# Layer 0's attention: each head's scaling and output transposes emitted inside the next head's tiles

## The chip, the core and the metric

The kernel runs on one core of a Trainium2 chip. The core has five engines that work side by side, each from a queue of its own: TensorE (PE, with its weight loads as PEld), VectorE (DVE), ScalarE (ACT), GpSimd (POOL) and SyncE (SP). They wait for each other through semaphores, and DMA engines move data between HBM, where the inputs lie, and the on-chip memory (SBUF). TensorE writes its results to PSUM. The metric is the device time of one execution in microseconds, the median of several runs.

## The reference, cut to what matters

The program is a two-layer backbone over 256 context and 512 latent tokens (T = 768, D = 1024). Layer 0 mixes tokens with two head groups side by side: four heads of differential attention, and four heads of a gated delta rule (GDN). The change lies in the attention heads and in what is done beside them:

```python
def _diff_attend(q, k, v, lam):
    s = jnp.einsum('bqhmd,bkhmd->bhmqk', q, k).astype(jnp.float32) * (A_HD ** -0.5)
    p = jax.nn.softmax(s, axis=-1)
    w = p[:, :, 0] - lam * p[:, :, 1]
    return jnp.einsum('bhqk,bkhe->bqhe', w.astype(v.dtype), v)

def merge(oa, ob, gate, ref):
    ya = (_rmsnorm(oa, subln_g) * (1.0 - lam_init)).reshape(bsz, n, A_V)
    yb = (_rmsnorm(ob, out_g) * jax.nn.silu(gate)).reshape(bsz, n, B_W)
    return jnp.concatenate([ya.astype(ref.dtype), yb.astype(ref.dtype)], axis=-1) @ w_out
```

Each attention head has two score maps; their softmaxes are subtracted with weight lambda and multiplied with V. Each head's output is then RMS-normed over its 128 columns. The GDN heads' output is normed too and multiplied with a gate, and both groups go through one output projection. Context queries see only the 256 context keys, latent queries see all 768.

## The kernel before, in words

Activations are held feature-major: a tile of 128 features on the partitions and 768 tokens along the free axis. Float32 projections are made of three passes over a value split in a high and a low part (`mm3`, L346, L347, L349); the weight's split is made on the fly by `wload` (L333 ACT for the high part, L335 DVE or POOL for the low part).

`layer0_mixer` first runs the GDN, which leaves its output in `self.O`, then the q, k and V projections of attention, and then the part that is touched here. PSUM holds there three large buffers (tag `big`: the scores `sc`, the transposed output `oT`, a gate's projection `pj`, the broadcasts `hb`) and two small ones (`sml`: `pT`, `pav`, `hn`).

For each of the four heads `attn_load` (L989) brings q and k from DRAM with twelve DMAs on POOL's queue into tiles with twelve buffers, six for one head. `attn_head` (L615) then loops over six tiles of 128 queries, the four latent ones (768 keys) first and the two context ones (256 keys) behind. One tile is: scores of both maps on TensorE (L633, L634), their maximum on DVE (L635), the exponential with its sum on ACT (L637, into one of five `e` buffers), three DVE instructions that combine both maps (L639, L641, L642), six transposes on TensorE (L647) with copies on ACT (L648), six products with V (L651), and a copy to `ot` on ACT (L652). POOL copies the first map's reciprocal to `r0` (L640).

Behind the six tiles stands the head's scaling: squares on POOL (L654, into an `e` buffer), row sums on DVE (L655), two POOL multiplies with `r0`, `rpow` on DVE (L564: an inverse square root by three integer steps and four Newton rounds of three instructions), a POOL multiply (L659) and POOL's scaling pass over the whole head (L660). Then the output: six transposes on TensorE into `oT` (L663) and the split into high and low part on ACT and DVE (L666, L667).

Behind head 0 comes `headnorm` (L578) for the GDN output, in two sets of two heads: squares on ACT, row sums as 24 matmuls a set (L588), `rpow` on DVE, 24 broadcasts a set (L595). Then come gates 0 and 1, and behind head 1 gates 2 and 3: a projection of u (48 passes of `mm3` over 384 columns), a tanh on ACT (L1091), a combination on DVE (L1092) and a product into `self.O` on POOL (L1093). Head 2 is preceded by the split of the four finished O tiles (L381 ACT, L382 DVE). Behind head 3 the residual x is loaded and the output projection `out0` begins.

The framework gives each engine its queue: it takes the emitted order as priority and lets a later instruction go first where its own estimates say that the earlier one isn't ready; buffers of one tag are handed out in turn. On the chip each queue then runs in that fixed order.

Of the kernel before, what the change touches and what calls it, by code (L numbers as in the profile page):

```python
# [18 lines left out]
P = 128  # L19
D = 1024  # L20
KT = D // P
NC = 256
NL = 512
T = NC + NL
NCH = T // P
# [218 lines left out]
class K:  # L244
# [319 lines left out]
    def rpow(self, x):  # L564
        nc = self.nc
        n = x.shape[-1]
        w = self.nwt.tile([P, 2, n], F32, tag="nwt", name=self.nm("nwt"), bufs=2)
        y, t = w[:, 0, :], w[:, 1, :]
        I32 = mybir.dt.int32
        nc.vector.tensor_scalar(x, x, 1.0 / P, EPS, op0=ALU.mult, op1=ALU.add)  # L570
        nc.vector.tensor_scalar(t.bitcast(I32), x.bitcast(I32), 1, None, op0=ALU.logical_shift_right)
        nc.vector.tensor_scalar(y.bitcast(I32), t.bitcast(I32), -1, 0x5F3759DF, op0=ALU.mult, op1=ALU.add)
        for i in range(4):
            nc.vector.tensor_tensor(t, y, y, op=ALU.mult)
            nc.vector.scalar_tensor_tensor(t, t, -0.5, x, op0=ALU.mult, op1=ALU.mult)
            nc.vector.scalar_tensor_tensor(x if i == 3 else y, t, 1.5, y, op0=ALU.add, op1=ALU.mult)

    def headnorm(self, os, nrm, gain):  # L578
        nc = self.nc
# [32 lines left out]
        self.sg = self.small(1, "sg")  # L612
        nc.vector.tensor_scalar(self.sg, self.sm("subln"), 1.0 - lam_init, None, op0=ALU.mult)

    def attn_head(self, h, qk, Vh, ypool, pool, ae, **kw):  # L615
        nc = self.nc
        ident = self.c("ident")
        o = pool.tile([P, NCH, P], F32, tag="ot", name=self.nm("ot"), bufs=2)
        rs = pool.tile([P, 2, NCH], F32, tag="rs", name=self.nm("rs"), bufs=2)
        r0, ss = rs[:, 0, :], rs[:, 1, :]  # L620
        for qt in (2, 3, 4, 5, 0, 1):
            k1 = T if qt >= 2 else NC
            nkt = k1 // P
            wt = pool.tile([P, NCH, P], F32, tag="wT", name=self.nm("wT"), bufs=NWT)
            es = []
            st = pool.tile([P, 6], F32, tag="st", name=self.nm("st"), bufs=8)
            for m in range(2):
                ps = self.big("sc")
                q, k, kl = qk[3 * m:3 * m + 3]
                lq = q[:, qt * P:qt * P + P]  # L630
                for a in range(0, k1, 512):
                    b = min(a + 512, k1)
                    nc.tensor.matmul(ps[:, a:b], lq, k[:, a:b], start=True, stop=False)  # L633
                    nc.tensor.matmul(ps[:, a:b], lq, kl[:, a:b], start=False, stop=True)  # L634
                nc.vector.reduce_max(st[:, m:m + 1], ps[:, 0:k1], axis=AX.X, negate=True)  # L635
                e = ae.tile([P, T], F32, tag="e", name=self.nm("e"), bufs=NE)
                nc.scalar.activation(e[:, 0:k1], ps[:, 0:k1], AF.Exp, bias=st[:, m:m + 1], accum_out=st[:, 2 + m:3 + m])  # L637
                es.append(e)
            nc.vector.reciprocal(st[:, 4:6], st[:, 2:4])  # L639
            nc.gpsimd.tensor_copy(r0[:, qt:qt + 1], st[:, 4:5])  # L640
            nc.vector.tensor_scalar(st[:, 5:6], st[:, 5:6], st[:, 2:3], self.nlam, op0=ALU.mult, op1=ALU.mult)  # L641
            nc.vector.scalar_tensor_tensor(es[0][:, 0:k1], es[1][:, 0:k1], st[:, 5:6], es[0][:, 0:k1], op0=ALU.mult, op1=ALU.add)  # L642
            for g in range(0, nkt, 3):
                gn = min(3, nkt - g)
                pt = self.sml("pT")
                for j in range(gn):
                    nc.tensor.transpose(pt[:, j * P:j * P + P], es[0][:, (g + j) * P:(g + j + 1) * P], ident)  # L647
                nc.scalar.activation(wt[:, g:g + gn, :], pt[:, 0:gn * P].rearrange("p (a b) -> p a b", a=gn), AF.Copy)  # L648
            po = self.sml("pav")
            for kt in range(nkt):  # L650
                nc.tensor.matmul(po[:, 0:P], wt[:, kt, :], Vh[:, kt * P:kt * P + P], start=kt == 0, stop=kt == nkt - 1)  # L651
            nc.scalar.activation(o[:, qt, :], po[:, 0:P], AF.Copy)  # L652
        sq = ae.tile([P, T], F32, tag="e", name=self.nm("sq"), bufs=NE).rearrange("p (a b) -> p a b", a=NCH)
        nc.gpsimd.tensor_tensor(sq, o, o, op=ALU.mult)  # L654
        nc.vector.tensor_reduce(ss, sq, axis=AX.X, op=ALU.add)  # L655
        nc.gpsimd.tensor_tensor(ss, ss, r0, op=ALU.mult)
        nc.gpsimd.tensor_tensor(ss, ss, r0, op=ALU.mult)
        self.rpow(ss)
        nc.gpsimd.tensor_tensor(ss, ss, r0, op=ALU.mult)  # L659
        nc.gpsimd.tensor_tensor(o, o, ss.unsqueeze(2).to_broadcast([P, NCH, P]), op=ALU.mult)  # L660
        pb = self.acc("oT", halves=True)
        for c in range(NCH):
            nc.tensor.transpose(pb[:, c * P:c * P + P], o[:, c, :], ident)  # L663
        yh = self.slot([P, T], F32R, "h", ypool, **kw)
# [351 lines left out]
    def layer0_mixer(self):  # L1016
        nc, tc = self.nc, self.tc
        w0 = self.ap["w0"]
        with ExitStack() as es:
# [52 lines left out]
            with self.psum("ps1", big=3, sml=2), tc.tile_pool(name="at", bufs=1, reuse_waits="tile") as at, \  # L1072
                    tc.tile_pool(name="ae", bufs=1, reuse_waits="tile") as ae:
                self.nwt = at
                ya = []
                yt = lambda tag, n, pool=at: pool.tile([P, T], F32, tag=tag, name=self.nm(tag), bufs=n)
                yt2 = lambda tag: at.tile([P, 2, T], F32, tag=tag, name=self.nm(tag), bufs=1)
                hg = self.small(1, "hg")
                nc.vector.tensor_scalar(hg, self.sm("gnorm"), 0.5, None, op0=ALU.mult)
                for h in range(4):  # L1080
                    qk = self.attn_load(h, at)
                    if h == 2:
                        ya += [self.split(self.O[:, i, :], pool=self.sp) for i in range(4)]
# [12 lines left out]

# [280 lines left out]
AD0 = 1  # L1377
AD1 = 7
OH = 0
GATES = ((0, 1), (2, 3), (), ())  # L1380
NQK = 12
NE = 5
NWT = 3
# [39 lines left out]
```

## Time and profile before

| | us |
|---|---|
| median of three runs | 2017.19 |
| lowest and highest run | 2016.58, 2025.78 |
| the profiled execution, its own time | 2019.74 |
| span of the profiled execution, first to last instruction | 2017.9 |
| mean granted clock of TensorE | 0.939 |
| layer 0's attention stage in the span | 512.2 to 703.6 |

Times in the trace are counted from the span's start. "Busy" is the time in which an engine works on an instruction. A granted clock of 1.00 is TensorE's higher level, 2.4 GHz, and 0.5 its lower one, 1.2 GHz; a stretch with both has a value between them. A wait is put down to the instruction that released it.

### The profile page before, as it was taken

The numbers are of one execution on the slowest core, as the hardware profiler recorded it, in microseconds if no ns is written. First come the engines' busy times: TensorE is split into PE (matmuls) and PEld (weight loads), VectorE is DVE, ScalarE is ACT, GpSimd is POOL, SyncE is SP. The second block draws the span as 40 slices with busy tenths as digits, with TensorE's granted clock in tenths as the row PEclk, the third lists the DMA queues.
The fourth block names the chain that finished last, engine by engine and source line by source line (L and its number), as shares of the span: only waits on it lengthen the run. The fifth ranks groups of instructions, "written<-read, shape, count | busy, mean of one in ns | idle before, by whom it ended". The sixth has DMA issues, their size and how long they took to land. (4 is left out here: it accounts for less than half of the span.)

```text
span 2017.9 us, 27188 instructions
## 1 busy us (share of the span) xinstructions
PE 1826.2 (90%) x10129; PEld 1599.8 (79%) x10129; DVE 1299.4 (64%) x2440; ACT 878.0 (44%) x1630; POOL 522.8 (26%) x410
## 2 busy tenths in 40 slices
PE   7588898989787698999999999989888999999997
PEld 2477788888686487999999999967566688888887
DVE  4898887985455437665765544677666685555556
ACT  4355543343434335442333242365666464333344
POOL 1545312221322114322222222233121331111112
PEclk9788977997798799999999999989999999999998
DMA  8433222222523024333344344333000242333324
GB/s 313 136 125 112 79 92 84 84 97 56 132 57 100 0 84 126 117 94 103 126 136 146 105 131 131 100 99 110 27 21 17 70 129 86 113 94 94 94 79 121
DMA packets 75669, 202.87 MB, mean 101 GB/s; under 512 B 8545, under 2 KB 18961, under 8 KB 75153
## 3 DMA queue, kind: packets, MB, share of 16 engines
q1 hardware_dynamic: 65984, 173.01, 27.4%
q10 hardware_dynamic: 4752, 16.85, 2.5%
q0 software_dynamic: 4800, 11.28, 2.5%
q8 instruction: 80, 1.31, 0.3%
q14 instruction: 53, 0.43, 0.1%
HBM read 189.28 MB, written 9.99 MB: 99 GB/s over the span
## 5 line engine op out<-in xcount | busy, mean ns | idle before, releaser
L333 ACT ACTIVATE hi<-raw 128x512 fp32r<-128x512 f32 (+2 forms) x429 | 262.0, 616 | 461.0 <-PE pj L347 209.6
L346 PE MATMUL pj<-uh,hi 128*128 128x384 f32 (+1 forms) x1248 | 437.1, 350 | 16.5 <-DVE cv L435 11.6
L347 PE MATMUL pj<-ul,hi 128*128 128x384 f32 (+1 forms) x1248 | 435.3, 349 | 0.0
L335 POOL TENSOR_TENSOR lo<-raw,hi 128x512 fp32r<-128x512 f32 (+1 forms) x143 | 193.7, 1354 | 725.1 <-ACT hi L333 687.6
L349 PE MATMUL pj<-uh,lo 128*128 128x384 f32 (+1 forms) x1248 | 344.5, 350 | 1.8 <-DVE lo L335 0.9
L335 DVE TENSOR_TENSOR lo<-raw,hi 128x512 fp32r<-128x512 f32 (+2 forms) x286 | 209.7, 737 | 166.6 <-ACT hi L333 156.1
L346 PEld LDWEIGHTS pj<-uh,hi 128*128 128x128 f32 x1248 | 243.4, 195 | 22.0 <-issue 16.5
L347 PEld LDWEIGHTS pj<-ul,hi 128*128 128x128 f32 x1248 | 243.4, 195 | 3.2 <-issue 0.8
L349 PEld LDWEIGHTS pj<-uh,lo 128*128 128x128 f32 x1248 | 233.5, 195 | 7.2 <-POOL lo L335 1.8
L435 DVE SCALAR_TENSOR_TENSOR y<-pj,smt,y 128x511 f32<-128x511 f32 (+1 forms) x264 | 161.6, 655 | 58.6 <-ACT y L425 56.1
L346 PE MATMUL dn<-h,hi 128*128 128x384 f32 (+2 forms) x560 | 193.0, 345 | 2.8 <-ACT hi L333 2.3
L347 PE MATMUL dn<-l,hi 128*128 128x384 f32 (+2 forms) x560 | 192.5, 344 | 0.0
L349 PE MATMUL dn<-h,lo 128*128 128x384 f32 (+2 forms) x560 | 168.2, 344 | 1.5 <-DVE lo L335 1.2
L560 DVE SCALAR_TENSOR_TENSOR x<-dn,mod,x 128x512 f32<-128x512 f32 (+1 forms) x152 | 93.0, 633 | 87.2 <-PE dn L349 87.1
L346 PE MATMUL pj<-u,hi 128*128 128x512 f32 x336 | 130.7, 389 | 0.0
L347 PE MATMUL pj<-u,hi 128*128 128x512 f32 x336 | 130.7, 389 | 0.0
L349 PE MATMUL pj<-u,lo 128*128 128x512 f32 x336 | 130.7, 389 | 0.0
L520 ACT ACTIVATE srow<-srow 128x1024 f32<-128x1024 f32 x56 | 59.3, 1059 | 154.2 <-POOL srow L519 149.3
L519 POOL TENSOR_TENSOR srow<-ada1w,srow 128x1024 f32<-128x1024 f32 x32 | 79.1, 2473 | 177.0 <-DMA ada1w<-in_ada 126.0
L346 PEld LDWEIGHTS dn<-h,hi 128*128 128x128 f32 x560 | 105.7, 189 | 10.6 <-ACT hi L333 3.7
L347 PEld LDWEIGHTS dn<-l,hi 128*128 128x128 f32 x560 | 105.7, 189 | 7.0 <-issue 0.5
L349 PEld LDWEIGHTS dn<-h,lo 128*128 128x128 f32 x560 | 103.5, 189 | 9.3 <-DVE lo L335 1.7
(410 smaller groups left out, 3351.2 us busy)
## 6 DMA issues: line engine op xcount, KB each, us to landing
raw<-in_wu SPq DMA_DIRECT2D x88, 512.0 KB, 3.6
ada1w<-in_ada SPq DMA_DIRECT2D x48, 512.0 KB, 3.6
raw<-in_w SPq DMA_DIRECT2D x38, 512.0 KB, 3.7
raw<-in_wd SPq DMA_DIRECT2D x72, 256.0 KB, 2.7
adaw<-in_ada0t ACTq DMA_DIRECT2D x24, 512.0 KB, 3.6
qk<-qdr POOLq DMA_DIRECT2D x48, 192.0 KB, 3.3
adaw<-in_ada SPq DMA_DIRECT2D x16, 512.0 KB, 7.6
raw<-in_w0o SPq DMA_DIRECT2D x16, 512.0 KB, 3.6
```

What stands on the lines that cost most here:

```text
L333: nc.scalar.activation(hi, raw[:, a:b], AF.Copy)
L335: eng.tensor_tensor(lo, raw[:, a:b], hi.bitcast(F32), op=ALU.subtract)
L346: nc.tensor.matmul(ps, hi[n], xh[:, a:b], start=n == 0, stop=False)
L347: nc.tensor.matmul(ps, hi[n], xl[:, a:b], start=False, stop=False)
L349: nc.tensor.matmul(ps, lo[n], xh[:, a:b], start=False, stop=n == last)
L435: nc.vector.scalar_tensor_tensor(y[:, o0:o1], ps[:, o0 + s:o1 + s], taps[i], y[:, o0:o1], op0=ALU.mult, op1=ALU.add)
L519: nc.gpsimd.tensor_tensor(junk, raw, self.srow[:, 0, :], op=ALU.mult)
L520: nc.scalar.activation(junk, junk, AF.Copy, accum_out=col(0))
L560: nc.vector.scalar_tensor_tensor(xs[m][:, a:b], ps[:, a:b], self.mod[l][0 if a >= NC else 1][:, 8 * mi + m:8 * mi + m + 1], xs[m][:, a:b], ...
```

## The change

`attn_head` is cut in three: `attn_tile` (one tile of queries), `attn_scale` and `attn_out`. Head h's scaling is emitted behind the second tile of head h + 1, its transposes and output split behind the fourth. Head 3's follow behind the loop. q and k of head h + 1 are loaded ahead of head h's tiles. One gate each stands behind heads 0 and 1, and gates 2 and 3 behind head 2; the split of O moves ahead of head 3. In the scaling, POOL's copies of `r0` go (the reciprocal is written to `rs` at once), the three small POOL multiplies move to DVE, and `rpow` makes three Newton rounds, in `headnorm` too.

```diff
-        for i in range(4):
+        for i in range(3):
             nc.vector.tensor_tensor(t, y, y, op=ALU.mult)
             nc.vector.scalar_tensor_tensor(t, t, -0.5, x, op0=ALU.mult, op1=ALU.mult)
-            nc.vector.scalar_tensor_tensor(x if i == 3 else y, t, 1.5, y, op0=ALU.add, op1=ALU.mult)
+            nc.vector.scalar_tensor_tensor(x if i == 2 else y, t, 1.5, y, op0=ALU.add, op1=ALU.mult)
...
-    def attn_head(self, h, qk, Vh, ypool, pool, ae, **kw):
-        rs = pool.tile([P, 2, NCH], F32, tag="rs", name=self.nm("rs"), bufs=2)
-        r0, ss = rs[:, 0, :], rs[:, 1, :]
-        for qt in (2, 3, 4, 5, 0, 1):
...
-            nc.vector.reciprocal(st[:, 4:6], st[:, 2:4])
-            nc.gpsimd.tensor_copy(r0[:, qt:qt + 1], st[:, 4:5])
-            nc.vector.tensor_scalar(st[:, 5:6], st[:, 5:6], st[:, 2:3], self.nlam, op0=ALU.mult, op1=ALU.mult)
-            nc.vector.scalar_tensor_tensor(es[0][:, 0:k1], es[1][:, 0:k1], st[:, 5:6], es[0][:, 0:k1], op0=ALU.mult, op1=ALU.add)
...
+    def attn_tile(self, qt, qk, Vh, o, rs, pool, ae):
...
+        nc.vector.reciprocal(rs[:, qt, :], st[:, 2:4])
+        nc.vector.tensor_scalar(st[:, 4:5], rs[:, qt, 1:2], st[:, 2:3], self.nlam, op0=ALU.mult, op1=ALU.mult)
+        nc.vector.scalar_tensor_tensor(es[0][:, 0:k1], es[1][:, 0:k1], st[:, 4:5], es[0][:, 0:k1], op0=ALU.mult, op1=ALU.add)
...
+    def attn_scale(self, o, rs, pool, ae):
+        nc = self.nc
+        r0 = rs[:, :, 0]
+        f = pool.tile([P, NCH], F32, tag="st", name=self.nm("f"), bufs=8)
         sq = ae.tile([P, T], F32, tag="e", name=self.nm("sq"), bufs=NE).rearrange("p (a b) -> p a b", a=NCH)
         nc.gpsimd.tensor_tensor(sq, o, o, op=ALU.mult)
-        nc.vector.tensor_reduce(ss, sq, axis=AX.X, op=ALU.add)
-        nc.gpsimd.tensor_tensor(ss, ss, r0, op=ALU.mult)
-        nc.gpsimd.tensor_tensor(ss, ss, r0, op=ALU.mult)
-        self.rpow(ss)
-        nc.gpsimd.tensor_tensor(ss, ss, r0, op=ALU.mult)
-        nc.gpsimd.tensor_tensor(o, o, ss.unsqueeze(2).to_broadcast([P, NCH, P]), op=ALU.mult)
+        nc.vector.tensor_reduce(f, sq, axis=AX.X, op=ALU.add)
+        nc.vector.tensor_tensor(f, f, r0, op=ALU.mult)
+        nc.vector.tensor_tensor(f, f, r0, op=ALU.mult)
+        self.rpow(f)
+        nc.vector.tensor_tensor(f, f, r0, op=ALU.mult)
+        nc.gpsimd.tensor_tensor(o, o, f.unsqueeze(2).to_broadcast([P, NCH, P]), op=ALU.mult)
+
+    def attn_out(self, o, ypool, **kw):
+        nc = self.nc
         pb = self.acc("oT", halves=True)
         for c in range(NCH):
-            nc.tensor.transpose(pb[:, c * P:c * P + P], o[:, c, :], ident)
+            nc.tensor.transpose(pb[:, c * P:c * P + P], o[:, c, :], self.c("ident"))
         yh = self.slot([P, T], F32R, "h", ypool, **kw)
         yl = self.slot([P, T], F32R, "l", ypool, **kw)
         nc.scalar.activation(yh, pb, AF.Copy, scale=self.sg)
...
+                qk2 = self.attn_load(0, at)
                 for h in range(4):
-                    qk = self.attn_load(h, at)
-                    if h == 2:
+                    if h == 3:
                         ya += [self.split(self.O[:, i, :], pool=self.sp) for i in range(4)]
-                    ya.append(self.attn_head(h, qk, V[h], ae if h < 2 else self.sp, at, ae, **({"bufs": 4} if h < 2 else {})))
+                    qk, qk2 = qk2, self.attn_load(h + 1, at) if h < 3 else None
+                    o = at.tile([P, NCH, P], F32, tag="ot", name=self.nm("ot"), bufs=2)
+                    rs = at.tile([P, NCH, 2], F32, tag="rs", name=self.nm("rs"), bufs=2)
+                    for n, qt in enumerate((2, 3, 4, 5, 0, 1)):
+                        self.attn_tile(qt, qk, V[h], o, rs, at, ae)
+                        if h and n == 1:
+                            self.attn_scale(*prev, at, ae)
+                        if h and n == 3:
+                            ya.append(self.attn_out(prev[0], *((self.sp,) if h > 2 else (ae,)), **({} if h > 2 else {"bufs": 4})))
+                    prev = o, rs
                     if h == OH:
                         for i in (0, 2):
                             self.headnorm([self.O[:, i + k, :] for k in range(2)], yt2("nrm"), hg)
...
                         nc.scalar.activation(gt, ps, AF.Tanh, scale=0.5)
                         nc.vector.scalar_tensor_tensor(gt, gt, 1.0, ps, op0=ALU.add, op1=ALU.mult)
                         nc.gpsimd.tensor_tensor(self.O[:, j, :], self.O[:, j, :], gt, op=ALU.mult)
+                self.attn_scale(*prev, at, ae)
+                ya.append(self.attn_out(prev[0], self.sp))
                 xs = self.loadx(self.sp)
                 nb = Norm(self, xs, lambda sh, dt, nm: yt("e", NE, ae), NS[1])
 
...
-GATES = ((0, 1), (2, 3), (), ())
+GATES = ((0,), (1,), (2, 3), ())
```

## Rows read from the trace of the kernel before

**Rows 1.** The page's busy times by engine, whole span.

```profile
PE 1826.2 (90%) x10129; PEld 1599.8 (79%) x10129; DVE 1299.4 (64%) x2440; ACT 878.0 (44%) x1630; POOL 522.8 (26%) x410
```

**Rows 2.** Attention stage by stretch: length; PE, PEld, DVE, ACT, POOL busy; clock; DMA.

```profile
512.20:542.30 30.10, 21.88 (x129) 18.43 (x127) 15.88 (x30) 15.33 (x41) 11.12 (x26) 0.83 0.72 163
542.30:565.30 23.00, 16.36 (x105) 16.19 (x103) 12.66 (x52) 2.75 (x4) 6.69 (x11) 0.63 0.24 55
565.30:582.00 16.70, 16.70 (x99) 16.70 (x98) 3.35 (x4) 2.72 (x5) 3.13 (x2) 1.00 0.11 33
582.00:605.10 23.10, 19.70 (x126) 15.94 (x124) 15.96 (x31) 16.18 (x41) 8.81 (x16) 1.00 0.37 92
605.10:615.60 10.50, 1.63 (x9) 1.45 (x8) 3.51 (x16) 0.28 (x1) 5.61 (x9) 0.55 0.32 75
615.60:634.10 18.50, 18.50 (x98) 18.50 (x98) 3.36 (x4) 3.60 (x6) 3.14 (x2) 0.89 0.10 29
634.10:660.80 26.70, 19.86 (x125) 16.65 (x124) 20.93 (x36) 18.97 (x45) 3.59 (x7) 0.94 0.39 138
660.80:670.40 9.60, 1.30 (x8) 1.17 (x7) 3.46 (x16) 0.28 (x1) 3.54 (x5) 0.67 0.00 0
670.40:694.30 23.90, 21.84 (x126) 17.46 (x124) 16.02 (x31) 15.99 (x41) 1.11 (x6) 0.92 0.00 1
694.30:703.60 9.30, 1.12 (x5) 1.12 (x6) 3.46 (x16) 0.20 (x1) 3.54 (x5) 0.53 0.00 0
512.20:703.60 191.40, 138.87 (x810) 123.61 (x809) 98.58 (x236) 76.29 (x183) 50.28 (x89) 0.83 0.28 73
```

**Rows 3.** TensorE's waits, 500 to 745 us (total, times, longest).

```profile
PE oT L663 <- POOL ot L660: 31.2, 4, 8.9
```

**Rows 4.** Timeline behind the last head, 694 to 706 us (start, length).

```profile
694.57 1.47 POOL L654 TENSOR_TENSOR sq<-ot 128x768 f32<-128x768 f32 x1 [5.92 <-ACT ot L652]
696.07 0.95 DVE L655 TENSOR_REDUCE rs<-sq 128x6 f32<-128x768 f32 x1 [6.84 <-POOL sq L654]
697.62 0.17 DVE L570 TENSOR_SCALAR rs<-rs 128x6 f32<-128x6 f32 x1 [0.59 <-POOL rs L657]
700.44 0.17 DVE L576 SCALAR_TENSOR_TENSOR rs<-nwt 128x6 f32<-128x6 f32 x1
700.96 1.47 POOL L660 TENSOR_TENSOR ot<-ot,rs 128x768 f32<-128x768 f32 x1
702.48 1.54 PE L663 MATMUL oT<-cst,ot 128*128 128x128 f32 x6 [8.30 <-POOL ot L660]
704.06 0.90 ACT L666 ACTIVATE h<-oT,sg 128x768 fp32r<-128x768 f32 x1 [9.56 <-PE oT L663]
704.99 1.02 DVE L667 SCALAR_TENSOR_TENSOR l<-oT,sg,h 128x768 fp32r<-128x768 f32 x1 [4.39 <-ACT h L666]
```

**Rows 5.** Timeline of the stretch behind head 0, 542 to 566 us.

```profile
542.26 2.94 PE L588 MATMUL hn<-cst,nrm 128*128 128x1 f32 x24
546.13 5.28 PE L588 MATMUL hn<-cst,nrm 128*128 128x1 f32 x24 [0.93 <-ACT nrm L585]
555.17 1.94 DVE L574 TENSOR_TENSOR nwt<-nwt 128x12 f32<-128x12 f32 x1
555.58 1.49 POOL L660 TENSOR_TENSOR ot<-ot,rs 128x768 f32<-128x768 f32 x1
557.12 1.54 PE L663 MATMUL oT<-cst,ot 128*128 128x128 f32 x6 [5.71 <-POOL ot L660]
558.46 7.08 PE L595 MATMUL hb<-cst,hst 128*128 128x128 f32 x48
```

**Rows 6.** Timeline of POOL and DVE inside head 1, 584 to 597 us.

```profile
584.82 1.84 POOL L1093 TENSOR_TENSOR O<-O,gt 128x768 f32<-128x768 f32 x1 [0.95 <-DVE gt L1092]
585.86 1.82 DVE L635 TENSOR_REDUCE st<-sc 128x1 f32<-128x768 f32 x2 [0.25 <-PE sc L634]
595.87 0.57 POOL L998 DMA_DIRECT2D qk<-qdr  x1 [2.79 <-PE sc L634]
```

More of the change, by code (lines that the diff above doesn't have):

```diff
@@ L613, in lam_prep @@
         nc.vector.tensor_scalar(self.sg, self.sm("subln"), 1.0 - lam_init, None, op0=ALU.mult)
-    def attn_head(self, h, qk, Vh, ypool, pool, ae, **kw):
+    def attn_tile(self, qt, qk, Vh, o, rs, pool, ae):
         nc = self.nc
         ident = self.c("ident")
-        o = pool.tile([P, NCH, P], F32, tag="ot", name=self.nm("ot"), bufs=2)
-        rs = pool.tile([P, 2, NCH], F32, tag="rs", name=self.nm("rs"), bufs=2)
-        r0, ss = rs[:, 0, :], rs[:, 1, :]
-        for qt in (2, 3, 4, 5, 0, 1):
[L622 to L638, printed above, removed]
-            nc.vector.reciprocal(st[:, 4:6], st[:, 2:4])
-            nc.gpsimd.tensor_copy(r0[:, qt:qt + 1], st[:, 4:5])
-            nc.vector.tensor_scalar(st[:, 5:6], st[:, 5:6], st[:, 2:3], self.nlam, op0=ALU.mult, op1=ALU.mult)
-            nc.vector.scalar_tensor_tensor(es[0][:, 0:k1], es[1][:, 0:k1], st[:, 5:6], es[0][:, 0:k1], op0=ALU.mult, op1=ALU.add)
[L643 to L652, printed above, removed]
@@ new lines, in attn_tile @@
+        k1 = T if qt >= 2 else NC
+        nkt = k1 // P
+        wt = pool.tile([P, NCH, P], F32, tag="wT", name=self.nm("wT"), bufs=NWT)
+        es = []
+        st = pool.tile([P, 6], F32, tag="st", name=self.nm("st"), bufs=8)
+        for m in range(2):
+            ps = self.big("sc")
+            q, k, kl = qk[3 * m:3 * m + 3]
+            lq = q[:, qt * P:qt * P + P]
+            for a in range(0, k1, 512):
+                b = min(a + 512, k1)
+                nc.tensor.matmul(ps[:, a:b], lq, k[:, a:b], start=True, stop=False)
+                nc.tensor.matmul(ps[:, a:b], lq, kl[:, a:b], start=False, stop=True)
+            nc.vector.reduce_max(st[:, m:m + 1], ps[:, 0:k1], axis=AX.X, negate=True)
+            e = ae.tile([P, T], F32, tag="e", name=self.nm("e"), bufs=NE)
+            nc.scalar.activation(e[:, 0:k1], ps[:, 0:k1], AF.Exp, bias=st[:, m:m + 1], accum_out=st[:, 2 + m:3 + m])
+            es.append(e)
@@ new lines, in attn_tile @@
+        nc.vector.reciprocal(rs[:, qt, :], st[:, 2:4])
+        nc.vector.tensor_scalar(st[:, 4:5], rs[:, qt, 1:2], st[:, 2:3], self.nlam, op0=ALU.mult, op1=ALU.mult)
+        nc.vector.scalar_tensor_tensor(es[0][:, 0:k1], es[1][:, 0:k1], st[:, 4:5], es[0][:, 0:k1], op0=ALU.mult, op1=ALU.add)
+        for g in range(0, nkt, 3):
+            gn = min(3, nkt - g)
+            pt = self.sml("pT")
+            for j in range(gn):
+                nc.tensor.transpose(pt[:, j * P:j * P + P], es[0][:, (g + j) * P:(g + j + 1) * P], ident)
+            nc.scalar.activation(wt[:, g:g + gn, :], pt[:, 0:gn * P].rearrange("p (a b) -> p a b", a=gn), AF.Copy)
@@ L653, in attn_head @@
+        po = self.sml("pav")
+        for kt in range(nkt):
+            nc.tensor.matmul(po[:, 0:P], wt[:, kt, :], Vh[:, kt * P:kt * P + P], start=kt == 0, stop=kt == nkt - 1)
+        nc.scalar.activation(o[:, qt, :], po[:, 0:P], AF.Copy)
+    def attn_scale(self, o, rs, pool, ae):
+        nc = self.nc
+        r0 = rs[:, :, 0]
+        f = pool.tile([P, NCH], F32, tag="st", name=self.nm("f"), bufs=8)
         sq = ae.tile([P, T], F32, tag="e", name=self.nm("sq"), bufs=NE).rearrange("p (a b) -> p a b", a=NCH)
```

## The prediction

> **What bounds the kernel now.** I read four views, from wide to narrow. The busy times say that TensorE is the engine that counts: 90% of the span, VectorE 64% [rows 1]. So a change pays where TensorE stands still, and every us taken from it here arrives at the end, because the stages behind this one keep it as busy. Next, the same busy times for the attention stage alone, cut by hand at the places where TensorE's work changes [rows 2]: 191.4 us, TensorE busy for 138.9, granted clock 0.83. The ten stretches are, in order: head 0's tiles (30.1), the head norm with head 0's output transposes (23.0), gates 0 and 1 (16.7), head 1's tiles (23.1), head 1's scaling (10.5), gates 2 and 3 (18.5), head 2's tiles (26.7), its scaling (9.6), head 3's tiles (23.9), its scaling (9.3). In the scaling stretches TensorE does 1.1 to 1.6 us of work, in the gates it is never idle. Third, TensorE's waits: 31.2 us in four waits of the oT transposes for POOL's scaled head [rows 3]; no other wait of the stage comes near. Fourth, the timeline of one such wait [rows 4]: square on POOL (1.47), row sums on DVE (0.95), POOL multiplies, fifteen small DVE instructions from 697.62 to 700.61 at 0.20 each, POOL again, POOL's scaling pass (1.47), and at 702.48 the transposes, 8.3 us after TensorE stopped. It is one serial chain over two engines, and TensorE's queue holds oT in front of everything else.
>
> **The change, part by part.**
>
> *The three inner chains leave TensorE's queue.* Heads 0 to 2 get their scaling emitted behind tile 1 of the next head and their transposes behind tile 3. The stretches of 10.5 and 9.6 [rows 2] go whole: -20.1. Their six transposes come back inside the next head: 1.5 us at the lower clock [rows 4], half that at the higher; I take 1.0 for each of three heads: +3.0. In front of oT there now lie a gate and two to four tiles, so the chain (about 8 us by [rows 4]) has cover: a gate is 16.7/2 = 8.35 us of pure TensorE work in which DVE is busy for 3.35/2 = 1.7 us [rows 2]. If the cover is gone, see the slow rival.
>
> *Head norm.* Its second set of row sums ends at 551.4, its broadcasts start at 558.46; between lie the oT wait and the transposes [rows 5]. Without head 0's scaling, the broadcasts wait only for the second set's power: a copy and now 12 instructions (three Newton rounds, not four) at 0.20, from 551.45 to about 554.1. That saves 558.46 - 554.1 = 4.4. Ends: 1.3, if the scaling is still woven in there and only the transposes go; 7.1, if the first set's broadcasts start at 551.4 (that set's sums end at 545.2, so its power could be there at about 548). I take 4.4, the middle of the three.
>
> *Gates.* One behind head 0, one behind head 1, two behind head 2. The work is the same; 18.5 us at clock 0.89 against 16.7 at 1.00 [rows 2] says that the 10.5 us pause before it cost 1.8. With that pause gone: -1.8. Each gate's DVE, ACT and POOL work stays beside TensorE's.
>
> *The split of O* moves from head 2's start to head 3's. Head 2 takes 26.7 against head 1's 23.1, with DVE busy 20.9 against 16.0 [rows 2]; the 3.6 move along: 0. Head 3's 23.9 falls to head 1's 23.1 without the pause in front of it: -0.8. The loads of x and the output weights come after u is free, a head later than now, but still a head (over 20 us) before their first use: 0.
>
> *Loads of q and k.* Head 2's are already issued while head 1's tiles run [rows 6], and no wait for a later head's load stands in TensorE's list. Being a head ahead buys nothing: 0. What is queued behind them on POOL is the square; TensorE does not wait for it at that point.
>
> *The POOL copies of r0* (24) and the POOL multiplies go; DVE has three more small instructions per head. Unhidden only behind head 3: three Newton instructions fewer (-0.6) and fewer crossings, POOL's two multiplies taking 697.02 to 697.62 against 2 x 0.20, the last one 700.61 to 700.96 against 0.20 plus a crossing [rows 4]: about -0.3. Together -0.9; 9.3 becomes 8.4.
>
> *What the heads pay.* Inside the next head DVE gets 0.95 + 15 x 0.20 + 1.02 = 5.0 us, ACT 0.9 [rows 4]; an e buffer (one of five) is held for the square, 1.47 + 0.95 = 2.4 us; and oT takes one of three large PSUM buffers that the scores rotate through. The trace shows none of this inside a head. Lower end 0: head 1 leaves DVE 23.1 - 16.0 = 7.1 us idle [rows 2], more than the 5.0, and a list-like planner would put most of the chain under the gate. A gain I exclude, since nothing is removed there. Upper end for the forecast 4 per head. I take 2: the transposes' own copies (1.0 and 0.9) cannot lie under the gate, the rest mostly can. +6.0.
>
> Before that last term the sum is -20.1 + 3.0 - 4.4 - 1.8 - 0.8 - 0.9 = -25.0; with it -19.0. Check by stretches: 30.1 + 18.6 + 33.4 + 3 x 26.1 + 3.6 + 8.4 = 172.4 against 191.4. The profiled execution took 2019.74 us (span 2017.9), 2.55 over the median of 2017.19; from the median the forecast is **1998.2 us**. The own range is 1990 (heads pay 0, head norm 7.1) to 2007 (heads pay 4, head norm 1.3).
>
> **A row and a rule that speak against it.** A DVE multiply of 12 columns took 1.94 us, against 0.17 for small DVE instructions elsewhere [rows 4], while POOL's scaling pass ran from 555.58 to 557.07 [rows 5]; a DVE maximum that reads PSUM was not held by a POOL pass (two in 1.82 us, [rows 6]). So some DVE instructions wait for POOL, and the change puts POOL's two long passes beside the softmax instead of into a pause. The Trainium skill (Advanced Engine Details and Errata, VectorE Performance Modes) says: "The second Vector SBUF port is shared with GPSIMD, so GPSIMD instructions and 2p Vector instructions will interfere/block eachother". By that rule each pass would be paid on DVE inside the heads; the trace's 1.94 us agrees in kind, and no row shows a softmax instruction beside such a pass. The sum by the rule would be that of POOL's rival below, by the rows alone it stays.
>
> **The rivals.**
>
> *Better (1986).* Heads pay nothing, the head norm gives 7.1, and the gates also fill the heads' drains, which I put at a third of head 1's 3.4 us of idle TensorE time (23.1 - 19.7 [rows 2]), three times: -25.0 - 2.7 - 3.4 = -31.1. For: DVE's 7.1 idle us. Against: the planner weaves by estimates, and the three score buffers stay.
>
> *POOL's passes hold DVE (2007).* Each inner head pays 1.47 + 1.47 on DVE on top: 3 x 2.9 = +8.8. For: the 1.94 us row. Against: passes under a gate meet a nearly idle DVE, and the maximum was not held.
>
> *The chain lands on the heads' path (2014).* DVE's 5.0 and the e buffer's 2.4 are all paid: 3 x 7.4 = 22.2 against 25.0. For: DVE, ACT and TensorE are all busy for 16 to 20 us of head 1's 23.1 [rows 2], so there is little slack in any of them. Against: the gate's 8.35 us.
>
> *Nothing moves (about 2014).* The emitted order is an input to a planner that orders each queue; it might leave the chains ahead of the gates as now, and only the small savings remain. Against: the transposes' place in TensorE's queue follows the text today.
>
> *Slower (2035).* oT stands in TensorE's queue inside a head, where a wait also stops the scores behind it. If the chain begins only behind tile 1's softmax, because its square queues for an e buffer or behind POOL's loads, and shares DVE with two tiles, the old 8.9 us wait [rows 3] reappears there. Each time the head must then fill again (head 1's idle TensorE time, 23.1 - 19.7 = 3.4) at the lower clock (head 3's TensorE work of 21.8 against 19.7: 2.1). 3 x 14.4 = 43.2 against 25.0: +18.2. It turns slower where oT waits over 25.0/3 - 5.5 = 2.8 us per head. Against: the chain needs 8 us and has a gate and up to four tiles.
>
> **How the numbers follow.** Forecast 0.46, better 0.13, POOL's passes 0.11, on the path 0.14, nothing moves 0.05, slower 0.11. About 0.5% (10 us) is what a measurement of this kernel tells from no change: below 2007 lie the forecast, the better case and half of the POOL case, 0.65; within it 0.24; above it 0.11. The range 1984 to 2015 leaves out the slow case and little else.
>
> **What would show it.** Right: the wait of oT for POOL falls from 31.2 to about 8 us, all behind head 3; the gates run at clock 1.00; the heads' stretches grow by 2 to 4 us; the stage takes about 172 us. Wrong: waits of oT or of the scores inside heads 1 to 3, DVE instructions of 2 to 3 us beside POOL's passes, TensorE still idle between the head norm's sums and broadcasts beyond 3 us, or a stage shorter by 19 us with the span unchanged.

## The result

The changed kernel took 1995.65 us (median), the kernel before 2018.71 in the same comparison: a ratio of 0.9892, 95% interval 0.9866 to 0.9918, so some 22 us less (17 to 27). A second comparison gave 0.9909 (0.9880 to 0.9939). The forecast was 1998.2, with a chance of 0.65 for faster by over 0.5%.

The profiled execution has a span of 1993.3 us. The attention stage by stretch, cut as in [rows 2] (length; busy time of PE, PEld, DVE, ACT, POOL with instructions; granted clock; DMA share and rate). In order: head 0's tiles, the head norm, gate 0, head 1 with gate 1, head 2 with gates 2 and 3, head 3, the last head's scaling, the whole stage, and all that lies behind it:

```profile
505.60:536.20 30.60, 21.79 (x127) 18.52 (x126) 15.88 (x30) 15.41 (x41) 13.01 (x26) 0.78 0.86 172
536.20:552.90 16.70, 15.01 (x98) 14.84 (x97) 6.90 (x29) 1.86 (x3) 0.00 (x0) 0.69 0.28 53
552.90:561.40 8.50, 8.50 (x52) 8.50 (x51) 1.11 (x2) 0.73 (x2) 1.28 (x1) 1.00 0.01 2
561.40:594.00 32.60, 28.01 (x180) 24.41 (x179) 22.08 (x50) 18.18 (x45) 10.45 (x14) 1.00 0.38 83
594.00:636.30 42.30, 36.61 (x228) 32.69 (x228) 24.75 (x51) 20.11 (x48) 9.68 (x7) 1.00 0.10 30
636.30:670.40 34.10, 23.90 (x131) 19.31 (x129) 25.52 (x53) 20.43 (x47) 6.09 (x3) 0.83 0.30 108
670.40:679.10 8.70, 1.21 (x7) 1.22 (x7) 3.46 (x16) 0.27 (x1) 2.94 (x2) 0.50 0.00 0
505.60:679.10 173.50, 135.04 (x812) 119.49 (x810) 99.70 (x230) 76.99 (x183) 43.45 (x53) 0.87 0.34 80
679.10:1993.30 1314.20, 1256.28 (x6576) 1110.02 (x6574) 799.40 (x1267) 578.28 (x1060) 312.38 (x220) 0.98 0.32 98
```

The stage takes 173.5 us where it took 191.4 [rows 2]: 17.9 less. The same cut through the kernel before shows that nothing is given back or gained behind the stage, 1314.3 against 1314.2 us:

```profile
703.60:2017.90 1314.30, 1256.16 (x6576) 1109.80 (x6575) 799.37 (x1267) 577.17 (x1060) 312.64 (x220) 0.98 0.33 98
```

TensorE's waits from 495 to 745 us (total, times, longest), against the 31.2 us in four of [rows 3]:

```profile
PE oT L666 <- POOL ot L660: 9.6, 3, 7.5
PE sc L629 <- ACT e L633: 7.8, 8, 3.7
PE sc L629 <- issue: 6.2, 1, 6.2
PE sc L629 <- DVE gt L1104: 4.4, 3, 1.6
PE pT L642 <- DVE e L637: 2.5, 3, 1.2
```

Of the four waits of the transposes only the last head's (7.5) is left; two of 1.0 are new, inside heads 1 and 2. The single wait of 6.2 us stands at the start of head 0, behind its first four score matmuls. The kernel before has 5.6 us there, and in the kernel without scaling (below) the same wait, 4.9 us, is put down to the DMA of q and k. Every kernel here has this wait, of 4.3 to 6.5 us; the change does not touch it.

The two profiled spans differ by 24.6 us, not 17.9. The other 6.7 are no work of the change: the first score comes at 505.64 us here and at 512.29 before, although the work ahead of it is the same. The clock ahead of the stage decides it (three executions, the stretch ahead of the stage; the kernel before, the changed kernel, and the changed kernel profiled again):

```profile
490.00:503.00 13.00, 13.00 (x74) 10.79 (x73) 2.28 (x6) 1.19 (x2) 1.03 (x2) 0.50 0.13 32
```

```profile
490.00:497.00 7.00, 7.00 (x74) 5.85 (x73) 1.94 (x5) 1.19 (x2) 1.03 (x2) 1.00 0.25 59
```

```profile
490.00:505.00 15.00, 14.69 (x128) 13.07 (x128) 2.64 (x6) 4.46 (x10) 1.03 (x2) 0.51 0.14 26
```

The same 74 matmul records took 13.00 us at clock 0.50 and 7.00 at 1.00. In the second profile of the changed kernel the slow clock fell into this stretch too, and its first score came at 519.38. Of its 13.7 us, 6.3 had come about further ahead. So below I compare kernels by the time **from the first score to the end of the span**, which leaves this out, and give the ratio of the times beside it. The two profiles of the changed kernel differ by 1.4 us in this measure, and by 0.1 us from head 1's first score to the first output projection (117.7 and 117.6); differences below these are not told apart.

### The profile page after: what moved, and what is told of

It reads as the page before. It is cut to its first block, busy times and chain, and to the rows that moved or that the text cites. A ratio compares the mean times of both kernels' runs of the same rounds, so it can differ in the third digit from the quotient of the medians.

```text
span 1993.3 us, 27154 instructions
## 1 busy us (share of the span) xinstructions
PE 1813.7 (91%) x10129; PEld 1589.2 (80%) x10129; DVE 1300.9 (65%) x2434; ACT 880.2 (44%) x1630; POOL 516.4 (26%) x374
## 3 DMA queue, kind: packets, MB, share of 16 engines
q1 hardware_dynamic: 65984, 173.01, 27.8%
```

## The experiments

All of them share the work ahead of the stage. "Stage" is first score to first output projection.

| kernel | first score at | stage | first score to end | against before | ratio of times (95%) |
|---|---|---|---|---|---|
| before | 512.29 | 191.4 | 1505.6 | | 1 |
| changed | 505.64 | 173.4 | 1487.7 | -17.9 | 0.9892 (0.9866 to 0.9918) |
| changed, again | 519.38 | 172.3 | 1486.3 | -19.3 | 0.9909 (0.9880 to 0.9939) |
| place undone | 503.70 | 188.2 | 1501.5 | -4.1 | 0.9977 (0.9952 to 1.0002) |
| gates pairwise | 515.97 | 171.1 | 1487.2 | -18.4 | 0.9886 (0.9858 to 0.9914) |
| loads undone | 503.49 | 172.7 | 1488.0 | -17.6 | 0.9882 (0.9850 to 0.9914) |
| scaling under the gate | 521.68 | 161.0 | 1475.1 | -30.5 | 0.9863 (0.9837 to 0.9889) |
| no scaling, heads 0 to 2 | 515.94 | 159.4 | 1475.2 | -30.4 | 0.9840 (0.9814 to 0.9866) |
| its GpSimd half only | 508.48 | 163.5 | 1476.7 | -28.9 | 0.9847 (0.9822 to 0.9871) |
| its VectorE half only | 511.51 | 161.3 | 1475.6 | -30.0 | 0.9854 (0.9823 to 0.9885) |
| transposes a tile later | 521.10 | 173.8 | 1488.0 | -17.6 | 0.9928 (0.9908 to 0.9947) |
| last wait filled | 506.38 | | 1478.3 | -27.3 | 0.9842 (0.9816 to 0.9868) |
| both | 509.44 | | 1465.6 | -40.0 | 0.9827 (0.9801 to 0.9853) |
| both, split of O spread | 502.98 | | 1463.1 | -42.5 | 0.9781 (0.9756 to 0.9806) |

(With the last wait filled, output projections begin before the stage ends, so the stage has no such end.)

### The changed kernel again

> The changed kernel itself, as the yardstick of this chip: about 1995 us, 1% below the kernel before, with a stage of attention of some 174 us. Its profile is a second sample of the clock ahead of the stage: in the profiled run of the kernel before the granted clock stood at 0.50 from about 483 to 503 us and the stage began 6.6 us later than in the changed kernel's run, though the instructions up to there are the same. If that was chance, the start of the stage scatters between about 505 and 512 us over these profiles, whatever the kernel; if it belongs to the change, every kernel here that keeps the rest of the change starts near 505.

Measured: 1999.57 us; first score at 519.38. Over these profiles the first score scatters from 502.98 to 521.68, kernels that keep the change and the one that undoes its main part mixed, wider than I had put down. The same kernel gave 505.64 and 519.38: the clock ahead of the stage does not belong to the change.

### The place undone

```diff
                         self.attn_tile(qt, qk, V[h], o, rs, at, ae)
-                        if h and n == 1:
-                            self.attn_scale(*prev, at, ae)
-                        if h and n == 3:
-                            ya.append(self.attn_out(prev[0], ...))
-                    prev = o, rs
+                    self.attn_scale(o, rs, at, ae)
+                    ys.append(self.attn_out(o, ...))
```

> Each head's scaling and output transposes stand right behind the head's own tiles again; the gates stay spread, q and k stay one head ahead, and the reciprocal root and the small steps stay as the change has them. Theory (the gain is that the transposes no longer stand in TensorE's queue ahead of the chain that they wait for): the waits of the transposes come back to about 30 us in all, against 9.6, and the time rises by 13 to 18 us over the changed kernel, to about 2010. Rival (the spreading of the gates and the shorter chain bring the gain): within 5 us of the changed kernel.

Measured: 13.8 and 15.2 us more than the two profiles of the changed kernel; by the ratios 0.0068 of 2018, 13.7 us. TensorE's waits of this kernel:

```profile
PE oT L666 <- POOL ot L660: 27.4, 4, 7.6
PE sc L629 <- ACT e L633: 6.4, 11, 2.5
```

The four waits are back. The theory holds: the place in TensorE's queue is the gain. By stretch, from TensorE's timeline of both: head norm 21.0 against 16.7, head 1 with its scaling and gate 41.9 against 32.6, head 2 likewise 49.6 against 42.3, but head 3 27.8 against 34.1. So the place brought 20.9 us, and **head 3 gave 6.3 of them back**. The rest, some 4 us against the kernel before, belongs to what this kernel keeps; 2.0 of it show in the head norm stretch, which is built as before but with the shorter chain (21.0 against 23.0 [rows 2]), and the rest was not taken apart.

### The gates pairwise, the loads undone

```diff
-GATES = ((0,), (1,), (2, 3), ())
+GATES = ((0, 1), (2, 3), (), ())
...
-                    if h == 3:
+                    if h == 2:
```

> Gates 0 and 1 behind head 0, gates 2 and 3 behind head 1, none behind head 2, and the split of O ahead of head 2's output; the scaling stays inside the next head's tiles and the rest as changed. Theory (a gate's projection only fills the drain between two heads' tiles, and the chain lies beside the next head's tiles): heads 2 and 3 stand back to back with nothing between them and cost their own drain, about 6 us more there, while two gates at one boundary give back little; in all 0 to +6 us. Rival (the gates in the drain are the cover that hides the chain): waits of transposes inside head 3 of 5 us or more, and +10 us.

Measured: within 1 us of the changed kernel. Head 3, with no gate ahead of it, has no wait of the transposes, and the rival falls:

```profile
PE oT L666 <- POOL ot L660: 8.6, 2, 7.5
```

Spreading the gates bought nothing that shows.

```diff
-                qk2 = self.attn_load(0, at)
...
-                    qk, qk2 = qk2, self.attn_load(h + 1, at) if h < 3 else None
+                    qk = self.attn_load(h, at)
```

> Each head's q and k are loaded at the head of its own loop again; the rest as changed. Theory (the loads are hidden in either place, as the buffers come free and SP's queue is ahead): no difference, within 2 us. Rival (the loads now stand ahead of the scores and would be late): scores wait on a transfer at the start of heads 1 to 3, 3 to 6 us each.

Measured: 0.3 and 1.7 us more than the changed kernel from the first score to the end, and a ratio of 0.9882: no difference. No wait for a load stands in heads 1 to 3.

### The scaling under the gate

```diff
-                        if h and n == 1:
-                            self.attn_scale(*prev, at, ae)
...
                     if h == OH:
                         ... headnorm ...
+                    if h < 3:
+                        self.attn_scale(*prev, at, ae)
                     for j in GATES[h]:
```

> The scaling of heads 0 to 2 is queued right behind the head's own tiles, ahead of the gates' work on VectorE and GpSimd, as I had supposed that it would run; the output transposes stay behind the next head's fourth tile. Theory (the chain's place in VectorE's and GpSimd's queues matters where it meets other work: the two transposes' waits inside heads 1 and 2, 1 us each, go, and head 3's squares no longer lie beside the split of O, whose GpSimd passes took 2.48 and 2.18 us and after which TensorE stood for 3.68 us): 3 to 7 us less than the changed kernel. Rival (VectorE and GpSimd have slack in either place): within 2 us. Against it: the chain on VectorE ahead of the gate's product may hold the gate's PSUM buffer and so the next head's scores, up to 12 us a head on the path for 1 to 3 us each, which would make it 3 to 9 us slower.

Measured: 12.6 and 11.2 us less than the changed kernel from the first score to the end, more than any case I had put down. By the ratios it is 6 to 9 us, with intervals that overlap, so the size rests on the profiles. The same cut (head 0, head norm, gate 0, heads 1, 2 and 3):

```profile
521.70:551.10 29.40, 21.84 (x129) 18.66 (x126) 15.88 (x30) 15.34 (x41) 9.89 (x20) 0.83 0.82 167
551.10:567.80 16.70, 14.96 (x97) 14.79 (x96) 8.46 (x45) 1.86 (x3) 5.17 (x7) 0.69 0.29 60
567.80:576.20 8.40, 8.40 (x51) 8.40 (x50) 1.10 (x2) 0.66 (x2) 2.15 (x3) 1.00 0.11 25
576.20:607.00 30.80, 28.04 (x180) 24.66 (x179) 21.57 (x50) 18.00 (x45) 9.04 (x13) 1.00 0.38 88
607.00:645.60 38.60, 36.41 (x228) 32.95 (x227) 23.04 (x51) 19.93 (x48) 11.14 (x8) 1.00 0.11 33
645.60:673.90 28.30, 21.44 (x131) 18.25 (x130) 22.18 (x37) 19.79 (x46) 2.48 (x1) 0.88 0.36 131
```

Heads 1 to 3 take 30.8, 38.6 and 28.3 where they took 32.6, 42.3 and 34.1. TensorE's work in heads 1 and 2 is the same to 0.2 us, so there it is all standing time; in head 3, 2.5 of the 5.8 us are the same matmuls at a higher clock.

### What the heads pay for the chain

```diff
-                        if h and n == 1:
-                            self.attn_scale(*prev, at, ae)
```

> The scaling of heads 0 to 2 is left out altogether (squares, sums, reciprocal root and products), so their outputs go on unscaled; the last head keeps its scaling. It prices what the heads pay for the chain inside them. By my forecast 2 us a head, by the trace of the changed kernel nearer to 1 us for the heads 1 and 2 and about 4 us for head 3: 3 to 8 us less than the changed kernel. Rival (the chain is hidden altogether): within 2 us. Rival (GpSimd's passes hold VectorE in every head): 9 us or more.

Measured: 12.5 and 11.1 us less than the changed kernel. That is beyond my 3 to 8 us and in the range of the rival "GpSimd's passes hold VectorE", which the next two runs take up. From head 1's first score to the first output projection it takes 106.3 us against 117.7, and 106.4 with the scaling under the gate. So inside the heads the chain cost **11.4 us**, and under the gate it costs nothing that shows: the head norm with gate 0, where head 0's chain then lies, takes 25.2 us in both kernels too.

Where the heads paid it: TensorE's waits over 0.5 us in head 2, changed kernel:

```profile
PE sc L629 <- DVE gt L1104: 1.3, 1, 1.3
PE pT L642 <- DVE e L637: 1.2, 1, 1.2
PE oT L666 <- POOL ot L660: 1.0, 1, 1.0
PE pT L642 <- DVE nwt L576: 0.8, 1, 0.8
```

Without the chain the last three are gone or down to 0.2 (that kernel's list, head 2):

```profile
PE sc L629 <- DVE gt L1102: 1.3, 1, 1.3
PE sc L629 <- ACT e L633: 0.5, 2, 0.3
PE oT L666 <- ACT e L633: 0.2, 1, 0.2
PE pT L642 <- DVE e L637: 0.2, 1, 0.2
```

So the transposes of the tile (pT) wait for its product of exponentials, and the transposes of the head before (oT) wait for GpSimd's last product. The longest wait of pT, 1.2 us, has a cause of its own. The product ahead of it takes 2.65 us instead of 1.02, beside a weight split and the squares on GpSimd:

```profile
599.19 1.29 POOL L335 TENSOR_TENSOR lo<-raw,hi 128x512 fp32r<-128x512 f32 x1
600.07 2.65 DVE L637 SCALAR_TENSOR_TENSOR e<-e,st,e 128x768 f32<-128x768 f32 x1
600.43 1.46 POOL L654 TENSOR_TENSOR sq<-ot 128x768 f32<-128x768 f32 x1
602.78 0.88 PE L642 MATMUL pT<-cst,e 128*128 128x128 f32 x6 [1.25 <-DVE e L637]
608.69 1.02 DVE L637 SCALAR_TENSOR_TENSOR e<-e,st,e 128x768 f32<-128x768 f32 x1
```

Two more products, one each in heads 1 and 2, take 1.63 and 1.64 us beside GpSimd's scaling pass. The wait of 0.8 us stands behind a product that is not held (608.69), but has steps of the chain ahead of it in VectorE's queue.

In heads 1 and 2 TensorE works as long as without the chain (28.0 us in both kernels; 36.6 against 36.4), at clock 1.00 in both, so the 2.1 and 3.7 us that these heads lose are waiting. Of head 3's 5.7 us, 2.4 are the same 131 matmuls at a lower clock (busy for 23.9 us against 21.5), and the rest is waiting.

The chain itself, in head 1 of the changed kernel:

```profile
566.27 1.47 POOL L654 TENSOR_TENSOR sq<-ot 128x768 f32<-128x768 f32 x1
568.76 0.93 DVE L655 TENSOR_REDUCE f<-sq 128x6 f32<-128x768 f32 x1
577.81 0.17 DVE L659 TENSOR_TENSOR f<-f,rs 128x6 f32<-128x6 f32 x1
578.11 1.47 POOL L660 TENSOR_TENSOR ot<-ot,f 128x768 f32<-128x768 f32 x1 [10.37 <-issue]
579.63 0.88 PE L666 MATMUL oT<-cst,ot 128*128 128x128 f32 x6 [1.02 <-POOL ot L660]
```

It begins at 566.27, when the gate's matmuls have been over for 4.9 us, and takes 13.3 us instead of some 8 [rows 4], since its small steps are woven between the head's maxima and products.

### Its two halves

```diff
-                            self.attn_scale(*prev, at, ae)
+                            self.pool_only(*prev, at, ae)
...
+        nc.gpsimd.tensor_tensor(sq, o, o, op=ALU.mult)
+        nc.gpsimd.tensor_tensor(o, o, rs[:, :, 0].unsqueeze(2).to_broadcast([P, NCH, P]), op=ALU.mult)
```

> Of the scaling of heads 0 to 2 only GpSimd's two passes are left, at their place behind the next head's second tile: the squares, and a product with the reciprocal row sums, which are ready; the sums, the reciprocal root and all small VectorE steps are left out, so these heads' outputs are scaled wrongly. From the first score to the first output projection the changed kernel takes 172 to 173 us, the one without any scaling in these heads 159.4. Theory (GpSimd's passes hold VectorE back, above all beside the split of O): at least half of those 13 us comes back, 166 us or more. Rival (VectorE's own small steps in the head's queue are the cost): under 162 us.

Measured: 163.5 us for the stage, between the two expectations; but 2.8 of the 4.1 us over the kernel without the chain lie in head 0, which the edit does not touch. From head 1's first score it is 107.3 against 106.3, and from the first score to the end 1.5 us more. Where they run here, GpSimd's passes are not the cost. But they do not run where the changed kernel has them: the second follows the first at once (569.52 and 571.07 in head 1, 4.9 and 6.4 us behind the head's first score, where the changed kernel has 4.9 and 16.7). There they lie beside VectorE's maxima, and no product of exponentials in heads 1 and 2 is held. What the passes cost at the places where the changed kernel has them, this run does not price.

```diff
-                            self.attn_scale(*prev, at, ae)
+                            self.dve_only(*prev, at, ae)
...
+        nc.vector.tensor_reduce(f, o, axis=AX.X, op=ALU.add)
...      f times f, then the small steps and self.rpow(f) as they were
```

> The other half: of the scaling of heads 0 to 2 only VectorE's steps are left at their place (a sum over the output itself, since there are no squares, then the small steps of the reciprocal root); GpSimd's two passes are left out, and nothing is scaled. Theory (GpSimd's passes are the cost): under 163 us from the first score to the first output projection. Rival (VectorE's some 18 steps, woven into the head's own, delay its maxima and its exponentials, and TensorE's drain with them): 168 us or more. If both halves stay near 159, the cost is their coupling, the waits from one engine to the other.

Measured: 161.3 us; from head 1's first score 107.4, from the first score to the end 0.4 us over the kernel without the chain. VectorE's steps by themselves are not the cost either. (The 161.3 lies in the range that I had put down for GpSimd's passes, but the run before speaks against them alone.) As put down beforehand, that leaves the coupling: a chain that crosses the engines and is stretched by it, so that its passes meet the products, and the transposes that need its end.

### The transposes one tile later

```diff
-                        if h and n == 3:
+                        if h and n == 4:
```

> The changed kernel with one number altered: the output transposes of the head before stand behind the fifth tile instead of the fourth; the chain of the scaling stays where the change has it, inside the tiles. Of the two halves of the chain neither alone costs the heads more than about 1 us, the whole one 11 us. Theory (the cost is the transposes' wait in TensorE's queue for the last product of a chain that is stretched to some 12 us, with what stands behind them late and the clock lower after that): with the transposes later, the waits of 1.02 us go and 5 to 11 of the 11 us come back, 162 to 168 us from the first score to the first output projection. Rival (the interplay on VectorE, the head's steps between the chain's, is the cost): within 2 us of the changed kernel's 172 to 173 us.

Measured: 173.8 us, nothing gained; the theory falls in this form. The number is the rival's, but the run does not single the rival out, for the planner that orders the queues moved the chain too: in head 1 its last small step and GpSimd's product now read

```profile
592.60 0.15 DVE L659 TENSOR_TENSOR f<-f,rs 128x6 f32<-128x6 f32 x1
592.89 2.17 POOL L660 TENSOR_TENSOR ot<-ot,f 128x768 f32<-128x768 f32 x1 [11.21 <-issue]
595.12 0.44 PE L666 MATMUL oT<-cst,ot 128*128 128x128 f32 x2 [2.55 <-POOL ot L660]
```

and the wait is 2.55 us instead of 1.02; head 1 takes 34.3 us instead of 32.6, so 1.5 of wait cost 1.7 (the head's other waits add up to nearly the same). A wait of oT inside a head is thus paid about in full, but emitting it later did not remove it. Head 2 took 2.4 us more as well and head 3 2.2 us less. What the held products would give back by themselves, no run here settles.

### The last wait, both, and the split of O

```diff
                 self.attn_scale(*prev, at, ae)
+                pre = {m: self.proj_part(w0o[m], ya, SEGS0[0]) for m in range(2)}
                 ya.append(self.attn_out(prev[0], self.sp))
...
-                    ps = self.proj(self.ap["w0o"][m], ya, nm="wo", segs=[seg])
+                    if seg == SEGS0[0] and m in pre:
+                        ps = self.proj_rest(*pre[m], ya, seg)
+                    else:
+                        ps = self.proj(w0o[m], ya, nm="wo", segs=[seg])
```

> Ahead of the last head's output transposes, the first two output projections of layer 0 run over the seven inputs that are done (42 matmuls); their eighth follows when the transposes are through. The sum of the work is the same. Theory (the last chain's 7.5 us of TensorE's wait, with 8.8 us from the last tile to the stage's end, is the one wait that the change left on the path): 6 to 9 us less than the changed kernel. Rival (the weights or the PSUM buffers of these projections are late there, or the wait moves to the residual): within 2 us.

Measured: 9.4 and 8.0 us less than the changed kernel from the first score to the end; by the ratios 10 to 14. In the 8.70 us ahead of the projections' eighth input TensorE is busy for 6.85 at clock 1.00, where it was 1.21 at 0.50 in the last scaling's stretch:

```profile
671.00:679.70 8.70, 6.85 (x33) 5.20 (x32) 3.60 (x17) 1.53 (x2) 3.74 (x3) 1.00 0.00 0
```

> Both edits of the two runs before: the scaling queued behind the head's own tiles, and the first two output projections in the last chain's wait. If both theories hold, their gains add, since they lie in different stretches: 9 to 16 us less than the changed kernel, about 1981 to 1986.

Measured: 22.1 and 20.7 us less than the changed kernel from the first score to the end, about the sum of the two (12.6 + 9.4, 11.2 + 8.0) and more than the 9 to 16 put down; by the ratio of 0.9827 (0.9801 to 0.9853) it is 13 to 17.

```diff
-                    if h == 3:
-                        ya += [self.split(self.O[:, i, :], pool=self.sp) for i in range(4)]
...
+                        if h == 3 and n in (1, 2, 3, 4):
+                            yo.append(self.split(self.O[:, n - 1, :], pool=self.sp))
```

> Scaling under the gates and the last wait filled, as in the run with both, and the split of O spread over head 3, one of its four parts behind each of the tiles 2 to 5, where the others make all four ahead of the head's first tile. Theory (in the first tiles the split's VectorE parts, 0.95 us each and up to 1.72 us beside GpSimd's gate product, make TensorE stand 2.4 us, after which its clock falls): head 3 loses that wait, 28.3 us falls to 23 to 26, and 2 to 6 us are gained over the run with both. Rival (the parts are only moved, and later tiles wait for them instead): within 2 us.

Measured: 2.5 us less than both from the first score to the end, and a ratio of 0.9781 (0.9756 to 0.9806), the lowest here. Head 3 of "both" and of this one:

```profile
634.30:662.40 28.10, 22.61 (x140) 19.37 (x139) 22.18 (x37) 19.80 (x46) 2.47 (x1) 0.88 0.07 20
```

```profile
628.20:652.30 24.10, 20.80 (x141) 17.48 (x139) 20.64 (x37) 19.69 (x46) 1.84 (x1) 1.00 0.08 23
```

The wait of 2.4 us is gone and the clock stays at 1.00: 4.0 us less in head 3, of which the stretch behind it takes back 1.5 to 2.

## Why the prediction was right, and where it was not

**What bounds it, and that the gain arrives.** Right. The stage lost 17.9 us and the 1314 us behind it did not change.

**The three chains leave TensorE's queue, -20.1 with +3.0 for the transposes.** Right, and the reason too: undoing the place alone brings the waits back to 27.4 us.

**The head norm, -4.4.** Undersized: 23.0 [rows 2] became 16.7, 6.3 less, near the upper end of 7.1. I had let the broadcasts wait for the second set's power. In the trace they begin at 545.98, only 0.75 us after the second set's sums, while that power ends at 550.04: the first set's broadcasts need only the first set's. That was my upper end; I had taken the middle of three values.

**Gates, -1.8.** The clock is 1.00 from 552.9 to 636.3 as forecast. Where the gates are put is worth nothing by itself.

**The split of O, 0; head 3, -0.8.** Head 3 was to take 29.7 and took 34.1. Without the chain it takes 28.4, so the split itself was about as forecast; the excess is the chain's.

**Loads, 0.** Right for heads 1 to 3, shown by undoing them.

**The last chain, 8.4.** 8.7: the wait fell from 8.30 [rows 4] to 7.53 us.

**What the heads pay, +6.** This step failed in its mechanism. I let most of the chain run under the gate. In the trace GpSimd's squares begin at 566.27, 600.43 and 641.73, in each case behind the gate's product and inside the next head's tiles. The price was 11.4 us, nearly twice mine and half of the 22.2 of the rival "on the heads' path". That rival had the place right, but not the payers: VectorE's steps alone, and a held `e` buffer with GpSimd's passes alone, each cost about 1 us from head 1 on; the chain across both engines cost 11.4. Two of the signs that I had named for being wrong did show, waits of oT inside heads 1 and 2 (1.0 us each) and VectorE instructions of over 2 us beside GpSimd's passes (2.65 and 2.22). Put under the gate, as I had imagined it, the chain costs nothing.

**Why the sum held all the same.** Two things that I had kept for the better case offset it. Heads 1 to 3 without the chain take 106.3 - 3 x 8.35 (gates) - 8.7 = 72.5 us, where my stretches gave 75.9 (3 x 24.1 + 3.6): 3.4 us less. With oT out of the way the next gate's matmuls fill the drains of heads 1 and 2: in the kernel without the chain gate 1 begins at 587.40, and head 1's last product with V ends at 592.77. The head norm gave 1.9 more. So +5.4 - 3.4 - 1.9, with 0.5 in head 0 and 0.3 in the last chain, makes +0.9: the stage took 173.4 us against the 172.4 of the check by stretches. The forecast of -19.0 lies between the two profiles' -17.9 and -19.3, partly by cancellation.

**The rivals.** "GpSimd's passes hold VectorE", priced at 8.8, is worth 1.5 us at most when the passes stand alone beside maxima. In the changed kernel it does show: in three products of exponentials, 0.6 us longer in head 1, 1.6 and 0.6 in head 2, and where head 2's squares meet the split of O in head 3 (next section but one). It is thus a part of the 11.4 us; its share is open. "Slower" needed waits of oT over 2.8 us a head; they were 1.0. "Nothing moves" is excluded by the timeline.

## What to carry to other kernels

Taking a wait out of the critical engine's queue pays at once, but the chain that it waited for still has to run somewhere: look in the queues of the engines that it uses, not in the text, for what stands ahead of it there. Queued behind the next phase's first steps it costs that phase; queued ahead of a stretch in which only the critical engine works it costs nothing, and here that was worth another 11 to 13 us by the profiles (6 to 9 by the ratios) on top of the change's 18. Compare from a common point in the program when the clock ahead of it varies.

## What the hardware showed that I had not expected

**The clock ahead of the stage.** The granted clock is 0.50 or 1.00 there, 1.2 or 2.4 GHz. In the kernel before, TensorE had waited 1.96 us at 483.16 and then worked at 0.50 with no pause until 503; in the changed kernel it had waited 1.64 us at 483.98, and from 490 on the clock was 1.00. The length of the wait does not decide it. In the kernel with VectorE's half it was longer, 2.01 us until 489.86, and the clock was 1.00 from 493.4 on; with the scaling under the gate it was 1.63 us until 494.01, and from 496 to 513 the clock stood at 0.50, with TensorE busy throughout. The same instructions, and up to 18.7 us between the earliest and the latest first score; what decides is not known.

**GpSimd and VectorE lengthen each other.** The split of O in head 3 of the changed kernel:

```profile
639.12 0.95 DVE L382 TENSOR_TENSOR l<-O,h 128x768 fp32r<-128x768 f32 x1
639.29 2.48 POOL L1105 TENSOR_TENSOR O<-O,gt 128x768 f32<-128x768 f32 x1 [5.33 <-DVE gt L1104]
640.86 3.86 DVE L382 TENSOR_TENSOR l<-O,h 128x768 fp32r<-128x768 f32 x2
641.73 2.18 POOL L654 TENSOR_TENSOR sq<-ot 128x768 f32<-128x768 f32 x1
645.57 0.94 DVE L382 TENSOR_TENSOR l<-O,h 128x768 fp32r<-128x768 f32 x1
```

A subtraction takes 0.95 us alone; the two that follow each other from 640.86 take 3.86. On GpSimd's side the gate's product takes 2.48 us instead of 1.84 [rows 6] and the squares 2.18 instead of 1.47 [rows 4]. By their ends they go in turn: the gate's product ends at 641.77, the squares at 643.91, and the second subtraction 0.81 us behind them. A maximum that reads PSUM is not held (0.95 us from 639.99, beside the gate's product). The Trainium skill (Advanced Engine Details and Errata, VectorE Performance Modes) says that VectorE's second port to SBUF is shared with GpSimd, and that GpSimd's instructions and VectorE's two-port ("2p") ones block each other; the trace agrees that both sides wait. Whether these subtractions and products are two-port instructions, no run here shows.

The next tile's scores start late: TensorE stands 3.68 us until 646.73, against 2.54 without the squares there. This meeting alone is not what makes head 3 long, though. Head 3 without the chain, and with GpSimd's passes alone, where the squares meet the split in the same way and TensorE stands 3.8 us:

```profile
638.20:666.60 28.40, 21.50 (x131) 18.29 (x129) 22.18 (x37) 19.74 (x46) 2.48 (x1) 0.88 0.36 130
633.90:663.20 29.30, 20.88 (x131) 17.71 (x130) 23.80 (x37) 19.57 (x46) 6.68 (x3) 0.88 0.34 126
```

It is worth 0.9 us there, of the 5.7 that the whole chain costs head 3.
